# GpSimd's element-wise work moved to VectorE and ScalarE, which issue in the order of a trace-time clock

## The chip, the cores and the metric

The kernel runs on one core of a Trainium2 chip. Its time is the device time of one execution in microseconds (us); the lower the better. The engines are TensorE (PE, with its weight loads shown as PEld), VectorE (DVE), ScalarE (ACT), GpSimd (POOL) and SyncE (SP, which here issues most of the DMAs). In the instruction names `pb`, `pm` and `pt` are PSUM tiles, `s` is any of 69 SBUF slots of 128 x 512 float32, and `wst`, `whi`, `wlo` are a weight tile as loaded and its high and low halves.

## The reference

A decoder trunk of two layers on 512 tokens of width 1024. Each layer adds to the residual `h`, in this order, each after an RMS norm:

1. half a SwiGLU feed-forward of width 2816 (FFN1),
2. a mixer: one projection to 29 blocks of 128 columns, divided among a short gated convolution, HGRN2 (a gated linear recurrence, 6 heads of 64, in chunks of 64 tokens) and RWKV-7 (6 heads of 64), then an output projection,
3. cross-attention (4 heads) to 256 memory tokens,
4. a second half feed-forward (FFN2).

The parts of the mixer that the change touches:

```python
# RWKV-7: token shift, key, its normalisation, output
pf = pf + (p_prev - pf) * mu
kk = k * k_k
kk = kk / maximum(sqrt(sum(kk * kk)), 1e-12)
k  = k * (1 + (a - 1) * k_a)
state = state * w + (state @ -kk) outer (kk * a) + v outer k     # one token after the other
y = ((y - mean) * rsqrt(var + eps)) * ln_w + ln_b ; out = (y + bonus) * g
# HGRN2: gates
log_f = log_sigmoid(f) + log1p(lb * exp(min(-f, 80))) ; k = (1 - lb) * sigmoid(-f)
```

A final RMS norm ends the trunk. All is float32.

## The kernel before, in words

Activations lie with their features on the partitions, so a tile is 128 features of all 512 tokens. A product with a weight matrix is done in blocks of 128 output columns ("a weight product"). `load_w` (L413) loads a weight block by SP into `wst`; ACT copies it, rounded, into `whi`, and DVE forms the rest, `wlo`. For each of up to eight blocks of 128 inputs, three matmuls then run (high by high, high by low, low by high), so a product of 1024 inputs is 24 matmuls of 512 columns. `split` (L535) does the same to an activation: ACT makes the high part, DVE the low one.

The FFNs are a plain loop over such products (`ffn`, L640). `Norm.chunk` (L578) squares each finished block of `h` on ACT, adds it to a sum (on POOL, except in the first and the last norm) and splits the block for the next stage.

The mixer (`mix`, L1246) is a set of Python generators that are run side by side while the kernel is traced:

- `rw_inputs` (L767), one for each of three pairs of RWKV heads, makes decays, normalised keys and the products between tokens of a chunk. It ends with four DMAs of triangular blocks to DRAM (`Ad`) and marks its pair as done (`in0` to `in2`). `turned` (L726) transposes a tile in PE and copies it out of PSUM, here into `UV`.
- `rw_solve` (L906) loads all the blocks back (`G<-Ad`), inverts them on DVE by 60 small steps, stores the result (`Td<-G`), loads it back in 12 pieces (`s<-Td`) and completes it with matmuls; `rw_chain` then goes through the eight chunks one after the other with a state `S`, and `rw_post` normalises the result. These three run in sequence.
- `hgrn` does the three pairs of HGRN heads: `hg_gates` makes the decays, `hg_pair` the scores on six levels of a chunk (`scaled`, `scores`, `merge`). At its end it brings the parked `h` back from DRAM (`s<-hd`) and adds eight output products to the fill.
- `mem_normed` normalises the memory for cross-attention.
- The fill (`Fill`, L440) is a queue of weight products that need nothing of the generators: the 29 projections of the mixer, then keys and values of cross-attention.

`Fill.run` (L501) decides which of them issues next. A trace-time clock (`Clock`, L113) keeps, for each engine, the stretches in which it is taken to be busy, and for each buffer the time at which it is written and read, from a linear cost per operation; `Clock.pe` is PE's time. A generator yields a `Need`: tiles, keys of finished products, free slots (`room`) and free PSUM banks. One whose needs are met by the clock goes on; otherwise the fill does its next step of three matmuls. Those in the list `calm` (HGRN and the memory) are passed over while the clock sees more than 5 us of work on DVE beyond PE's time, and ask for three slots more.

PE's instructions are kept in the order in which they were traced (`tc.keep_in_program_order`). The order of the other engines, and of SP's queue, is chosen afterwards by the framework's own scheduler. Every engine then runs its instructions strictly in that fixed order on the chip. In the profile, all operations that go through the clock's wrapper have its line: L253 for DVE, ACT, POOL and DMAs, L302 for matmuls, L306 for transposes.

Of the kernel before, what the change touches and what calls it, by code (L numbers as in the profile page):

```python
# [17 lines left out]
SPACES = (bass.MemoryType.SB, bass.MemoryType.PSUM)  # L18

P = 128  # L20
# [59 lines left out]
class Slots:  # L80


    def __init__(self, pool, n):
        self.pool = pool
        self.free = deque(range(n))
        self.held = {}
        self.n = 0
        self.low = n

    def get(self, dt=F32):  # L90
        i = self.free.popleft()
        self.low = min(self.low, len(self.free))
        self.n += 1
        t = self.pool.tile([P, T], dt, name=f"s{i}_{self.n}", tag=f"s{i}", bufs=1)
        self.held[id(t)] = (i, t)
        return t
# [16 lines left out]
class Clock:  # L113
# [6 lines left out]
    def __init__(self):  # L120
        self.pe = 0.0
        self.mode = None
        self.func = None
        self.dma = 0.0
        self.busy = {e: [] for e in ("DVE", "ACT", "POOL")}
        self.buf = {}

# [5 lines left out]
    @staticmethod  # L133
    def box(x):
        if x.space not in SPACES:
# [14 lines left out]
    def last(self, name):  # L150
        return max((max(r[4], r[5]) for r in self.buf.get(name, ())), default=0.0)

# [34 lines left out]
    def note(self, engine, op, args, kw):  # L187
        aps = [x for x in args if type(x).__name__ == "AP"]
        outs = aps[:1] + [kw[k] for k in ("accum_out",) if k in kw]
        ins = aps[1:] + [v for k, v in kw.items() if k != "accum_out" and type(v).__name__ == "AP"]  # L190
        if op == "copy_predicated":
            ins.append(aps[0])
        t = max([self.when(x) for x in ins] + [self.when(x, True, engine == "PE") for x in outs]) + 0.06
        n = max(x.free_size() for x in (outs + ins)[:2])
        if engine == "PE":
            t = self.pe = max(self.pe, t - 0.06) + self.matmul(op, ins, kw)
            t += 0.2
        elif op == "dma_start":
            size = aps[0].size() * 4
            t = self.dma = max(t + 2.0, self.dma) + size / 300e3  # L200
        else:
            t = self.fit(engine, max(t, self.pe - 5), self.cost(engine, op, args, n, ins))
        for x in ins:
            self.use(x, t, False)
# [20 lines left out]
    def cost(self, engine, op, args, n, ins):  # L225
# [9 lines left out]
        if op == "tensor_tensor_scan":  # L235
            return 0.2 + 2.6e-3 * n
        if op == "copy_predicated":
            return 0.2 + 1.3e-3 * n
        return 0.17 + (1.5e-3 if op == "scalar_tensor_tensor" else 1.1e-3) * n


class Timed:
# [5 lines left out]
    def __getattr__(self, op):  # L248
# [3 lines left out]
        def call(*args, **kw):  # L252
            ins = fn(*args, **kw)  # L253
            clock.note(name, op, args, kw)
# [4 lines left out]
class Banks:  # L259
# [11 lines left out]
    def get(self, dt=F32):  # L271
        t = self.pool.tile(self.shape, dt, name=self.name, tag=self.name, bufs=self.n)
        i = len(self.names) - self.n
        if i >= 0:
            self.clock.use(t, self.clock.last(self.names[i]), False)
            self.clock.buf.pop(self.names[i], None)
# [6 lines left out]

class Need:


    def __init__(self, *aps, keys=(), room=0, banks=(), ahead=0.0):
        self.aps, self.keys, self.room, self.banks, self.ahead = aps, keys, room, banks, ahead


@with_exitstack
def trunk(ctx: ExitStack, tc: tile.TileContext, a, out, parts=("ffn1", "mix", "xa", "ffn2"), dbg=None):
# [30 lines left out]
    sl = Slots(spool, NSLOT)  # L323
# [25 lines left out]
    def send(key, t):  # L349

        away[key] = dram.tile([P, T], F32, name=key, tag=key)
# [58 lines left out]
    ve.tensor_scalar(oml, lbt, -1.0, 1.0, ALU.mult, ALU.add)  # L410

# [28 lines left out]
    class Fill:  # L440
# [60 lines left out]
        def run(self, *gens, calm=()):  # L501
# [9 lines left out]
            while todo:  # L511
                at = [ready(n, SPARE * c) for _, n, c in todo]
# [33 lines left out]
    def rms_sums(acc, n):  # L546
# [5 lines left out]
        r = tiny.tile([P, 4], F32, name="rms", tag="rms")  # L552
        ve.tensor_scalar(r[:, :k], ps[:, :k], 1.0 / D, EPS, ALU.mult, ALU.add)
        gp.tensor_tensor(r[:, :k], r[:, :k], mhalf.to_broadcast([P, k]), op=ALU.pow)
        rh = tiny.tile([P, 4], F32R, name="rmsh", tag="rmsh")
        rl = tiny.tile([P, 4], F32R, name="rmsl", tag="rmsl")
# [14 lines left out]
    class Norm:  # L571
# [6 lines left out]
        def chunk(self, d, adder=gp):  # L578
# [3 lines left out]
            else:  # L582
                sq = sl.get()
                se.activation(sq, h[d], AF.Square)
                adder.tensor_tensor(self.acc, self.acc, sq, op=ALU.add)
# [38 lines left out]
    def start(name, src):  # L624
# [10 lines left out]
        for d in range(ND):  # L635
            n.chunk(d, ve)
# [3 lines left out]
    def ffn(l, which, n, nxt, between=None):  # L640
# [13 lines left out]
        for f0, f1 in SLABS:  # L654
# [22 lines left out]
            for d in range(ND):  # L677
# [4 lines left out]
                if last:  # L682
                    nxt.chunk(d, ve if nxt.l is None else gp)
# [42 lines left out]
    def turned(x, low, dst):  # L726
# [4 lines left out]
        for hf in range(2):  # L731
# [12 lines left out]
            ve.tensor_copy(dst(high, 4 * hf + 1, 4 * hf + 1 + nw), pv[C:P, 0:nw, high, :])  # L744
            if hf:
                ve.tensor_copy(dst(high, 0, 1), pv[C:P, 3:4, high, :])
# [11 lines left out]
    def rw_shift(l, n, i, ps):  # L758
        t = evac(n, ps)
        dd = sl.get()  # L760
        gp.tensor_tensor(dd[:, 1:], t[:, :T - 1], t[:, 1:], op=ALU.subtract)
        gp.tensor_scalar(dd[:, 0:1], t[:, 0:1], -1.0, None, ALU.mult)
        ve.scalar_tensor_tensor(t, dd, col(l, "rwkv_mu", i), t, op0=ALU.mult, op1=ALU.add)
        sl.put(dd)
        return t

    def rw_inputs(l, n, st, p):  # L767
        UV, Z, lr, X = st["UV"], st["Z"], st["lr"], st["X"]
        cs = slice(p * P, (p + 1) * P)
        yield Need(keys=[(l, f"k{p}"), (l, "wa")], room=ROOMS[p])  # L770
# [15 lines left out]
        el = gp if p else ve  # L786
        el.tensor_tensor(lw, G, lw, op=ALU.subtract)

        kk = sl.get()
        ve.tensor_scalar(kk, k, col(l, "rwkv_k_k", p), None, ALU.mult)  # L790
# [14 lines left out]
        ve.tensor_scalar(t0, ag, 1.0, col(l, "rwkv_k_a", p), ALU.subtract, ALU.mult)  # L805
        ve.scalar_tensor_tensor(k, t0, 1.0, k, op0=ALU.add, op1=ALU.mult)
        el.tensor_tensor(ag, kk, ag, op=ALU.mult)
        pc = tiny.tile([P, NC_], F32, name="pc", tag=f"pc{p}", bufs=1)
        ve.tensor_copy(pc, c8(ep)[:, :, C - 1])
        st["pc"].append(pc)  # L810
        yield Need(keys=[(l, f"r{p}")], room=4)
        r = X[f"r{p}"]
        AR, BK, BKH, BKT = [], [], [], []
        for hf in range(2):
# [4 lines left out]
            gp.tensor_tensor(arv[:, :, 1, :], c8(r[:, tt]), c8(ep[:, tt]), op=ALU.mult)  # L819
# [3 lines left out]
            for j in range(2):  # L823
                js = half(j)
                ve.tensor_tensor(bkv[js, :, j, :], c8(ag[:, tt])[js], e[js], op=ALU.mult)
                gp.tensor_tensor(bkv[js, :, 1 - j, :], c8(k[:, tt])[js], e[js], op=ALU.mult)
            AR.append(ar)
            BK.append(bk)
        sl.put(lw, ag, kk, G)
# [5 lines left out]
        yield Need(room=5)  # L835
# [70 lines left out]
    def rw_solve(l, st):  # L906
# [6 lines left out]
        G = cpool.tile([P, H * H], F32, name="G", tag="G")  # L913
# [16 lines left out]
        sp.dma_start(Td, G[0:n, :])  # L930
        yield Need(room=6)
# [50 lines left out]
    def rw_chain(l, st):  # L982
# [13 lines left out]
        for c in range(NC_):  # L996
# [24 lines left out]
            if c < NC_ - 1:  # L1021
# [3 lines left out]
                S2 = tiny.tile([P, 3, C], F32, name="rwS", tag="rwS", bufs=3)  # L1025
# [17 lines left out]
    def rw_post(l, st, ys):  # L1043
# [17 lines left out]
        for p in range(3):  # L1061
# [3 lines left out]
            ve.tensor_scalar(y, y, col(l, "rwkv_ln_w", p), col(l, "rwkv_ln_b", p), ALU.mult, ALU.add)  # L1065
            gp.tensor_tensor(y, y, bon[p], op=ALU.add)
# [10 lines left out]
    def hg_gates(l, st, p):  # L1077
# [3 lines left out]
        x, m, e1, e2 = sl.get(), sl.get(), sl.get(), sl.get()  # L1081
        ve.tensor_scalar(x, f, -1.0, 80.0, ALU.mult, ALU.min)
# [3 lines left out]
        se.activation(e1, m, AF.Exp, scale=-1.0)  # L1086
        ve.tensor_tensor(x, x, m, op=ALU.subtract)
# [3 lines left out]
        se.activation(x, x, AF.Ln)  # L1091
        ve.scalar_tensor_tensor(e1, f, 0.0, e2, op0=ALU.min, op1=ALU.subtract)
        gp.tensor_tensor(m, m, x, op=ALU.add)
        gp.tensor_tensor(m, m, e1, op=ALU.add)

        k = sl.get()
        gp.tensor_tensor(k, e1, f, op=ALU.subtract)
        se.activation(k, k, AF.Exp)
        ve.tensor_scalar(k, k, oml[:, l, p:p + 1], None, ALU.mult)
# [503 lines left out]
```

## Time and profile before

| | |
|---|---|
| median of 3 runs | 2540.8 us (2539.44 to 2542.9) |
| the profiled execution | 2538.74 us, span 2536.9 us |
| granted TensorE clock, mean | 0.975 |
| busy: PE, DVE, ACT, POOL | 2436.8, 1405.4, 973.2, 271.1 us |
| HBM read and written | 228.39 MB and 12.06 MB |

The span runs from the first to the last instruction of the profiled execution. Stages by the span's time in us: FFN1 of layer 0 to about 383, its mixer to about 797, cross-attention to about 911, FFN2 and the FFN1 of layer 1 to about 1634, mixer to about 2046, cross-attention to about 2161, FFN2 and the last norm to the end.

An instruction's row gives line, engine, operation, output<-inputs, shape, count, busy time, mean ns of one, and the engine's idle time just before, with what ended it. A row of waits gives the waiting engine and tile, what released it, us in total, times, and the longest. A row of stretches gives start and end, length, for each engine its busy us and its instructions, then the granted clock as a share, the DMA engines' share and GB/s.

### The profile page before, as it was taken

To read this page: it belongs to the slowest core of one execution; us is meant where nothing else is said; L and a number is where in the kernel's file an instruction comes from. 1 tells how busy PE (TensorE), PEld (TensorE's weight loads), DVE (VectorE), ACT (ScalarE), POOL (GpSimd) and SP (SyncE) were. 2 spreads that over 40 slices of the span, in tenths; PEclk is the share of its full clock that TensorE was granted. 3 is DMA by queue.
4 is the path that set the end of the run, shared out by engine and by line. 5 is a ranking of instruction groups with operands and counts; after the bars stand their busy time and mean duration, and the time that the engine had idled before them with its cause. 6 is when DMAs were issued, how large, how long until landed. Compare 5 with 4: busy or idle time off the path is not lost.

```text
span 2536.9 us, 34159 instructions
## 1 busy us (share of the span) xinstructions
PE 2436.8 (96%) x13812; PEld 1993.4 (79%) x13812; DVE 1405.4 (55%) x2068; ACT 973.2 (38%) x1338; POOL 271.1 (11%) x250
## 2 busy tenths in 40 slices
PE   8999999799989999999999999988999899999997
PEld 6888887577868878888888888866877688788886
DVE  5444456777756554344554444576876566444444
ACT  4222235554554342222332222355454544322232
POOL 0000013411201010000100000243221111000000
PEclk9999999899999999999999999999999999999998
DMA  4333332134323133333323333412334222333322
GB/s 144 100 109 99 100 121 81 57 91 125 122 67 106 50 104 93 99 91 100 100 92 100 100 92 98 128 59 72 110 107 129 65 78 78 100 94 99 100 91 76
DMA packets 92012, 242.65 MB, mean 96 GB/s; under 512 B 21840, under 2 KB 24528, under 8 KB 91856
## 3 DMA queue, kind: packets, MB, share of 16 engines
q1 hardware_dynamic: 88544, 234.36, 29.9%
q10 hardware_dynamic: 3312, 6.12, 0.6%
q8 instruction: 109, 1.79, 0.3%
q14 instruction: 47, 0.39, 0.1%
HBM read 228.39 MB, written 12.06 MB: 95 GB/s over the span
## 4 chain that ended last, share of the span: by engine, by line
PE 82%; DVE 8%; ACT 4%; issue 3%; POOL 2%; DMA 1%; SPq 0%; DVEq 0%; ACTq 0%; POOLq 0%
PE pb L302 75%; DVE s L253 6%; PE pm L302 5%; ACT s L253 2%; POOL s L253 2%; PE pt L302 1%; ACT L253 1%; DVE wlo L253 1%; DVE G L253 1%; PE pm L306 1%; SPq L253 0%; DMA wst<-w_mix_in 0%; DMA hgate<-s 0%; ACT whi L253 0%; PE pt L306 0%
## 5 line engine op out<-in xcount | busy, mean ns | idle before, releaser
L302 PE MATMUL pb<-s,whi 128*128 128x512 f32 (+1 forms) x6160 | 1912.0, 392 | 22.3 <-DVE s L253 12.0
L302 PEld LDWEIGHTS pb<-s,whi 128*128 128x128 f32 x6160 | 1156.7, 191 | 276.1 <-issue 17.2
L302 PE MATMUL pb<-s,wlo 128*128 128x512 f32 (+1 forms) x3080 | 1196.8, 389 | 1.4 <-DVE wlo L253 1.4
L253 ACT ACTIVATE whi<-wst 128x1024 fp32r<-128x1024 f32 (+5 forms) x445 | 433.8, 976 | 1090.5 <-PE pb L302 735.9
L302 PEld LDWEIGHTS pb<-s,wlo 128*128 128x128 f32 x3080 | 586.6, 190 | 120.8 <-DVE wlo L253 3.4
L253 DVE TENSOR_TENSOR wlo<-wst,whi 128x1024 fp32r<-128x1024 f32 (+5 forms) x445 | 501.1, 1126 | 109.8 <-ACT whi L253 102.3
L253 DVE TENSOR_TENSOR s<-pb,s 128x512 f32<-128x512 f32 (+1 forms) x345 | 236.7, 689 | 524.5 <-PE pb L302 497.3
L253 ACT ACTIVATE s<-s 128x512 f32<-128x512 f32 (+2 forms) x458 | 284.4, 627 | 289.0 <-DVE s L253 229.0
L253 POOL TENSOR_TENSOR s<-s,s 128x512 f32<-128x512 f32 (+2 forms) x142 | 180.2, 1275 | 1591.1 <-ACT s L253 1348.8
L253 DVE TENSOR_TENSOR s<-s,s 128x512 f32<-128x512 f32 (+3 forms) x378 | 244.2, 655 | 77.0 <-ACT s L253 68.0
L253 DVE SCALAR_TENSOR_TENSOR s<-pb,s 128x512 f32<-128x512 f32 x96 | 66.4, 692 | 226.0 <-PE pb L302 226.0
L253 DVE SCALAR_TENSOR_TENSOR s<-s,vec,s 128x512 fp32r<-128x512 f32 (+2 forms) x100 | 115.9, 1161 | 36.9 <-POOL s L253 19.1
L253 ACT ACT_TABLE_LOAD x96 | 123.2, 1283 | 22.0 <-DVE s L253 17.3
L253 POOL TENSOR_TENSOR s<-s 128x256 f32<-128x256 f32 (+2 forms) x64 | 68.8, 1086 | 156.8 <-DVE s L253 98.3
L302 PEld LDWEIGHTS pm<-s,s 64*64 64x64 f32 (+2 forms) x1104 | 61.3, 156 | 18.4 <-issue 10.7
L302 PE MATMUL pm<-s,s 64*64 64x64 f32 (+2 forms) x1104 | 67.3, 246 | 8.4 <-ACT Z L253 3.4
L253 POOL TENSOR_TENSOR rms<-rms,mhalf 128x4 f32<-128x4 f32 (+1 forms) x10 | 10.4, 1040 | 449.6 <-DVE rms L253 449.6
L253 ACT ACTIVATE s<-s,vec 128x512 fp32r<-128x512 f32 (+1 forms) x72 | 50.9, 709 | 2.0 <-DMA s<-xT 2.0
L302 PE MATMUL pb<-whi,s 128*128 128x512 f32 x128 | 51.1, 441 | 0.0
L302 PEld LDWEIGHTS pm<-s 64*64 64x64 f32 (+1 forms) x1152 | 37.1, 140 | 8.6 <-issue 6.9
L302 PE MATMUL pm<-s 64*64 64x32 f32 (+1 forms) x1152 | 40.7, 224 | 0.0
L306 PE MATMUL pm<-cst,s 128*128 128x128 f32 x192 | 29.1, 294 | 6.7 <-ACT s L253 5.5
(105 smaller groups left out, 827.3 us busy)
## 6 DMA issues: line engine op xcount, KB each, us to landing
wst<-ffn_w_in SPq DMA_DIRECT2D x175, 512.0 KB, 3.5
wst<-w_mix_in SPq DMA_DIRECT2D x58, 512.0 KB, 3.5
wst<-ffn_w_out SPq DMA_DIRECT2D x64, 448.0 KB, 3.3
wst<-ffn_w_out SPq DMA_DIRECT2D x32, 512.0 KB, 3.5
wst<-xattn_wk SPq DMA_DIRECT2D x16, 512.0 KB, 3.5
wst<-xattn_wv SPq DMA_DIRECT2D x16, 512.0 KB, 3.7
wst<-xattn_wq SPq DMA_DIRECT2D x16, 512.0 KB, 3.4
wst<-xattn_wo SPq DMA_DIRECT2D x32, 256.0 KB, 2.6
```

Source lines behind the costliest of these rows:

```text
L253: ins = fn(*args, **kw)
L302: self.pin(nc.tensor.matmul(*args, **kw))
L306: self.pin(nc.tensor.transpose(*args, **kw))
```

## The change

1. *GpSimd's element-wise work.* All additions, subtractions and products of whole tiles go from POOL to DVE. POOL keeps the power of -0.5 of the norms' sums and the memsets.
2. *Fewer and other steps.* The token shift `t + (prev - t) * mu` is done as `t * (1 - mu)` on ACT and one multiply-add on DVE (`omu` is made once), without the two POOL steps. The key's norm is `exp(-0.5 * ln(max(sum, 1e-24)))` in place of square root, maximum, logarithm and exponential. `1 + (a - 1) * k_a` is one ACT step (`omka` is made once).
3. *DVE's work to ACT.* Scalings by a column (`k_k`, `1 - lb`, `hgrn_norm`), the affine step with `ln_w` and `ln_b`, and all PSUM copies of `turned` are done by ACT.
4. *The order.* The clock notes for each DVE and ACT instruction (ACT's DMA issues too) when it takes it to start; at the end `issue_in_order` sorts each engine's instructions by that time and chains them by manual dependencies. The clock is refined: new costs for DVE, reuse of buffers (`renew`), readers of one PSUM bank one after the other, DMAs fitted into gaps. The memory's loads are no longer kept in program order.
5. *Who waits.* `rw_inputs` joins the `calm` list, ahead of `hgrn`; `mem_normed` leaves it and asks for more slots. `hgrn`'s gates wait for `in2`, that is for all RWKV inputs, and yield in several places.

```diff
+def issue_in_order(tc, clock):
+    dep = mybir.DependencyInfo(mybir.DependencyClass.NoSync, mybir.DependencyReason.DATA)
+    for q in clock.queue.values():
+        q = [x[2].ins for x in sorted(q, key=lambda x: x[:2])]
+        for a, b in zip(q, q[1:]):
+            tc.add_manual_dep(b, a.name, dep, reason="issue_in_order")
...
         else:
-            t = self.fit(engine, max(t, self.pe - 5), self.cost(engine, op, args, n, ins))
+            cost = self.cost(engine, op, args, n, reads)
+            t = self.fit(engine, max(t, self.pe - 5), cost)
+            first = t - cost
+            t += 0.08
+            if engine in self.queue:
+                self.queue[engine].append((first, len(self.queue[engine]), ins))
...
-        return 0.17 + (1.5e-3 if op == "scalar_tensor_tensor" else 1.1e-3) * n
+        return 0.08 + (1.15e-3 if op == "scalar_tensor_tensor" else 1.05e-3) * n
...
     def rw_shift(l, n, i, ps):
         t = evac(n, ps)
-        dd = sl.get()
-        gp.tensor_tensor(dd[:, 1:], t[:, :T - 1], t[:, 1:], op=ALU.subtract)
-        gp.tensor_scalar(dd[:, 0:1], t[:, 0:1], -1.0, None, ALU.mult)
-        ve.scalar_tensor_tensor(t, dd, col(l, "rwkv_mu", i), t, op0=ALU.mult, op1=ALU.add)
-        sl.put(dd)
-        return t
+        x = sl.get()
+        se.activation(x, t, AF.Copy, scale=omu[:, l * 11 + i:l * 11 + i + 1])
+        ve.scalar_tensor_tensor(x[:, 1:], t[:, :T - 1], col(l, "rwkv_mu", i), x[:, 1:], op0=ALU.mult, op1=ALU.add)
+        sl.put(t)
+        return x
...
             se.copy(dst(low, 4 * hf, 4 * hf + 4), pv[0:C, :, low, :])
             nw = 3 + (hf == 0)
-            ve.tensor_copy(dst(high, 4 * hf + 1, 4 * hf + 1 + nw), pv[C:P, 0:nw, high, :])
+            se.copy(dst(high, 4 * hf + 1, 4 * hf + 1 + nw), pv[C:P, 0:nw, high, :])
...
         ps = head_sum(t0)
-        se.activation(t0, ps, AF.Sqrt)
-        ve.tensor_scalar(t0, t0, 1e-12, None, ALU.max)
+        ve.tensor_scalar(t0, ps, 1e-24, None, ALU.max)
         se.activation(t0, t0, AF.Ln)
-        se.activation(t0, t0, AF.Exp, scale=-1.0)
-        el.tensor_tensor(kk, kk, t0, op=ALU.mult)
+        se.activation(t0, t0, AF.Exp, scale=-0.5)
+        ve.tensor_tensor(kk, kk, t0, op=ALU.mult)
...
-            yield Need(keys=[(l, f"hg{p}")], room=11 if p == 2 else 7)
-            gates.append(hg_gates(l, st, p))
+            yield Need(keys=[(l, f"hg{p}"), (l, "in2")], room=11 if p == 2 else 7)
+            gates.append((yield from hg_gates(l, st, p)))
...
-            gp.tensor_tensor(wb[:, :, 1, :], bb[:, :, 1, :], ref, op=ALU.subtract)
+            ve.tensor_tensor(wb[:, :, 1, :], bb[:, :, 1, :], ref, op=ALU.subtract)
...
-        F.run(*[rw_inputs(l, n, st, p) for p in range(3)],
-              seq(rw_solve(l, st), rw_chain(l, st), rw_post(l, st, ya)), calm=(hgrn(), mem_normed()))
+        F.run(seq(rw_solve(l, st), rw_chain(l, st), rw_post(l, st, ya)), mem_normed(),
+              calm=[rw_inputs(l, n, st, p) for p in range(3)] + [hgrn()])
...
-        (gp if d % 3 == 2 else ve).tensor_tensor(n.scaled[d], n.scaled[d], n.rstd, op=ALU.mult)
+        ve.tensor_tensor(n.scaled[d], n.scaled[d], n.rstd, op=ALU.mult)
         (sp if d % 2 else se).dma_start(out[:, d, :], n.scaled[d])
+    issue_in_order(tc, clock)
```

More of the change, by code (lines that the diff above doesn't have):

```diff
@@ L80, with __init__ @@
 class Slots:
-    def __init__(self, pool, n):
+    def __init__(self, pool, n, clock):
         self.pool = pool
+        self.clock = clock
         self.free = deque(range(n))
@@ L94, in get @@
         t = self.pool.tile([P, T], dt, name=f"s{i}_{self.n}", tag=f"s{i}", bufs=1)
+        self.clock.renew(t, f"s{i}")
         self.held[id(t)] = (i, t)
@@ L123, in __init__ @@
         self.func = None
-        self.dma = 0.0
-        self.busy = {e: [] for e in ("DVE", "ACT", "POOL")}
+        self.busy = {e: [] for e in ("DVE", "ACT", "POOL", "DMA")}
         self.buf = {}
+        self.names = {}
+        self.fresh = set()
+        self.queue = {e: [] for e in ("DVE", "ACT")}
     @staticmethod
@@ L134, in box @@
     def box(x):
-        if x.space not in SPACES:
+        if x.space != bass.MemoryType.SB:
             return 0, INF, 0, INF
@@ L151, in last, with renew, tile @@
         return max((max(r[4], r[5]) for r in self.buf.get(name, ())), default=0.0)
+    def renew(self, x, old):
+        t = self.last(old)
+        self.buf.pop(old, None)
+        self.buf[self.key(x)] = [(0, INF, 0, INF, t, t)]
+        self.fresh.add(self.key(x))
+    def tile(self, pool, shape, dt, name, bufs):
+        t = pool.tile(shape, dt, name=name, tag=name, bufs=bufs)
+        names = self.names.setdefault(name, [])
+        names.append(t.name)
+        if len(names) > bufs:
+            self.renew(t, names[-1 - bufs])
+        return t
     def use(self, x, t, write):
@@ L253, in call @@
             ins = fn(*args, **kw)
-            clock.note(name, op, args, kw)
+            clock.note(name, op, args, kw, ins)
             return ins
@@ L271, in get @@
     def get(self, dt=F32):
[L272 to L276, printed above, removed]
+        t = self.clock.tile(self.pool, self.shape, dt, self.name, self.n)
         self.names.append(t.name)
@@ L349, in send @@
     def send(key, t):
-        away[key] = dram.tile([P, T], F32, name=key, tag=key)
+        away[key] = clock.tile(dram, [P, T], F32, key, 1)
         sp.dma_start(away[key], t)
@@ L410, in trunk @@
     ve.tensor_scalar(oml, lbt, -1.0, 1.0, ALU.mult, ALU.add)
+    omu = cpool.tile([P, 2 * 11], F32, name="omu", tag="omu")
+    for l in range(L):
+        o = l * VL + VOFF["rwkv_mu"]
+        ve.tensor_scalar(omu[:, l * 11:l * 11 + 11], vec[:, o:o + 11], -1.0, 1.0, ALU.mult, ALU.add)
+    omka = cpool.tile([P, 2 * 3], F32, name="omka", tag="omka")
+    for l in range(L):
+        o = l * VL + VOFF["rwkv_k_a"]
+        ve.tensor_scalar(omka[:, l * 3:l * 3 + 3], vec[:, o:o + 3], -1.0, 1.0, ALU.mult, ALU.add)
     def load_w(src, cols, piece=1024, between=None):
@@ L511, in run @@
             while todo:
-                at = [ready(n, SPARE * c) for _, n, c in todo]
+                at = [ready(n, SPARE * (c and n.spare)) for _, n, c in todo]
                 busy = clock.backlog("DVE") > CALM
@@ L930, in rw_solve @@
         sp.dma_start(Td, G[0:n, :])
+        F.done.add((l, "solved"))
         yield Need(room=6)
```

132 lines of the change are left out of this document (73 added, 59 removed).

## The prediction

> **What bounds the kernel now.** I read the page's head and its chain of work first, then the busy times by stage, the waits of TensorE (PE), and the timeline where its longest wait stands. The stages below are FFN, mix, cross-attention, two FFNs, mix, attention, FFN.
>
> ```profile
> span 2536.9 us, 34159 instructions
> PE 2436.8 (96%) x13812; PEld 1993.4 (79%) x13812; DVE 1405.4 (55%) x2068; ACT 973.2 (38%) x1338; POOL 271.1 (11%) x250
> ...
> PE 82%; DVE 8%; ACT 4%; issue 3%; POOL 2%; DMA 1%; SPq 0%; DVEq 0%; ACTq 0%; POOLq 0%
> ```
>
> ```profile
> 403.00:757.00 354.00, 319.60 (x2875) 251.87 (x2872) 250.15 (x460) 189.51 (x263) 85.69 (x86) 0.93 0.29 88
> 924.00:1654.00 730.00, 730.00 (x3237) 604.23 (x3236) 341.46 (x390) 216.46 (x265) 29.12 (x22) 1.00 0.32 99
> 1654.00:2006.00 352.00, 317.28 (x2873) 250.41 (x2871) 249.23 (x458) 189.11 (x263) 85.57 (x86) 0.93 0.29 89
> ```
>
> The columns after the stretch and its length are PE, weight loads, VectorE (DVE), ScalarE (ACT), GpSimd (POOL), then the granted clock. In the FFNs PE is busy 730.00 of 730.00 us at clock 1.00: nothing done on the other engines can shorten them. Only the two mixes are open: PE idles 354.00 - 319.60 = 34.4 us in the first and 34.7 us in the second, and the clock loses up to 0.07 x 354 = 25 us in each, some 10 of it inside the idle time itself (estimate: a little under a third of the idle at half clock). So 2 x (34.5 + 15) = 99 us is all that a perfect order could bring. Attention has only single waits of 1 us at its edges.
>
> Who ends PE's waits in the first mix (us in total, times, longest), in three windows, 403 to 500, 500 to 600, 600 to 757:
>
> ```profile
> PE pm L302 <- DVE UV L253: 10.1, 2, 8.6
> PE pm L306 <- ACT s L253: 2.8, 1, 2.8
> ...
> PE pm L302 <- ACT s L253: 4.6, 2, 4.1
> PE pm L302 <- ACT Z L253: 1.7, 1, 1.7
> ...
> PE pt L302 <- DVE s L253: 7.9, 2, 5.3
> PE pt L302 <- issue: 2.1, 1, 2.1
> ```
>
> (The 4.1 within the 4.6 straddles two windows and ends near 600; one more of 3.75 is shown below.) These are a few long waits, not many short ones. The longest, in the timeline:
>
> ```profile
> 444.13 2.12 DVE L253 SCALAR_TENSOR_TENSOR s<-s,s 128x256 f32<-128x256 f32 x2
> 446.33 3.43 POOL L253 TENSOR_TENSOR s<-s,s 64x256 f32<-64x256 f32 x4 [0.63 <-DVE s L253]
> 454.79 0.43 DVE L253 COPY UV<-pm 64x256 f32<-64x256 f32 x1
> 455.27 3.37 PE L302 MATMUL pm<-s,lr 64*128 64x512 f32 x4 [8.63 <-DVE UV L253]
> 456.00:463.00 7.00, 7.00 (x21) 3.80 (x21) 4.83 (x7) 5.58 (x7) 2.60 (x3) 0.56 0.14 32
> ```
>
> PE is pinned to the order of the trace-time clock. Its next matmul needs a PSUM bank that a 0.43 us copy on DVE frees, and that copy stands at 454.79, behind some 10 us of RWKV products that DVE shares with POOL. The order that DVE runs is not the order that PE's order was made for. Afterwards PE runs at 0.56 for 7 us, so the wait costs 8.6 + 3.1 us.
>
> **The change part by part.** The durations that price it (mean ns of one is the number after the busy time):
>
> ```profile
> L253 POOL TENSOR_TENSOR s<-s,s 128x512 f32<-128x512 f32 x106 | 151.0, 1428 | 1561.9 <-ACT s L253 1342.2 <-DVE s L253 219.2
> L253 POOL TENSOR_TENSOR s<-s 128x256 f32<-128x256 f32 x36 | 31.1, 876 | 100.6 <-PE pm L302 51.3 <-DVE s L253 42.0 <-PE pt L302 7.2
> L253 POOL TENSOR_TENSOR s<-s 128x511 f32<-128x511 f32 x22 | 29.2, 1328 | 43.7 <-DVE s L253 43.7
> L253 POOL TENSOR_TENSOR s<-s,s 64x256 f32<-64x256 f32 x24 | 19.8, 824 | 20.6 <-DVE s L253 19.2
> L253 DVE TENSOR_TENSOR s<-s,s 128x512 f32<-128x512 f32 x154 | 109.2, 712 | 54.1 <-ACT s L253 46.3
> L253 DVE TENSOR_TENSOR s<-s,s 128x256 f32<-128x256 f32 x72 | 29.3, 438 | 5.9 <-ACT s L253 5.9
> L253 DVE TENSOR_TENSOR s<-s,s 64x256 f32<-64x256 f32 x24 | 18.4, 767 | 0.2
> L253 DVE SCALAR_TENSOR_TENSOR s<-s,vec,s 128x512 fp32r<-128x512 f32 x64 | 86.5, 1354 | 17.1 <-ACT s L253 15.5
> L253 DVE TENSOR_SCALAR s<-s,vec 128x512 f32<-128x512 f32 x28 | 14.1, 505 | 12.0 <-POOL s L253 11.6
> L253 ACT ACTIVATE s<-s,vec 128x512 f32<-128x512 f32 x8 | 5.7, 710 | 0.0
> L253 ACT COPY s<-pm 64x256 f32<-64x256 f32 x24 | 8.2, 360 | 18.7 <-PE pm L306 16.1 <-PE pm L302 2.7
> L253 ACT ACT_TABLE_LOAD x96 | 123.2, 1283 | 22.0 <-DVE s L253 17.3
> ```
>
> *POOL to DVE.* 106 full-width and some 6 more of its products at 0.71 us make 80 us, and about 72 of 256 columns at 0.44 us make 32: DVE gets 112 us. *DVE to ACT.* 54 PSUM copies of the transposes (about 18 us in all at 0.22 to 0.43 each), 24 of the 28 scalings at 0.505 (12 us) and 6 more scalings go over: DVE loses some 35. *Contention.* Half-width products that take 438 ns at 256 columns take 767 while POOL runs its own 824; the 64 split steps, mostly beside POOL's sum of squares, take 1354 where a full-width product takes 712. With POOL silent that gives back 64 x 0.64 = 41, 24 x 0.33 = 8, and from the like forms about 20 more: some 70 us. So 112 - 35 - 70 leaves DVE at about 1412 us, as now; without any relief it would be 1405 + 77 = 1482, and with the mean of the undisturbed steps being lower still (the 712 and 438 hold some disturbed ones), some 1390. I take 1410.
>
> [...]
>
> *ACT.* 22 token shifts become one ACT scaling each (0.71) instead of 1.33 and a one-column step on POOL: 15.6 us; 18 scalings at 0.71 make 13; 12 affine steps, not in this trace, lie between 0.63 (a full-width step without operands, estimate from this 0.71) and 0.9, say 9; the copies, at 0.36 for the largest of three sizes, 16. Six Sqrt steps go, some 4 us, with between none and two table loads each, up to 12 x 1.28 = 15 us. ACT ends between 1008 and 1023, 40%: it does not bind, its latencies stand beside PE's fill work (each weight product is 24 matmuls, some 5.4 us).
>
> *The order.* DVE and ACT are chained in the order of the clock that also orders PE. It costs no instruction. What it can close is the wait between the two orders. Per mix: the UV wait (its copy is on ACT now) 8.6, of which I take 6, since DVE still has the same products to do, and its slow clock 3; the ACT and Z waits (2.8 + 1.7 and small ones, 6 in all) half, 3; the DVE waits of the state chain, where
>
> ```profile
> 654.15 2.65 DVE L253 TENSOR_TENSOR s<-s 128x256 f32<-128x256 f32 x3
> 658.46 0.34 DVE L253 TENSOR_TENSOR s<-Z,pt 128x192 f32<-128x192 f32 x1
> 653.00:667.00 14.00, 8.71 (x90) 7.79 (x88) 11.01 (x22) 5.49 (x9) 4.93 (x6) 0.63 0.33 111
> ```
>
> three HGRN subtractions at 0.88 beside POOL stand ahead of the 0.34 us addition that the chain needs, 5.3 + 2.1, half, 3.5, and 2.5 of 5 for the clock at 0.63. The wait of 4.1 stays, because its cause is elsewhere:
>
> ```profile
> 587.42 5.75 SPq L253 DMA_DIRECT2D s<-Td  x12
> 598.09 1.06 ACT L253 ACTIVATE whi<-wst 128x1024 fp32r<-128x1024 f32 x1 [2.51 <-DMA wst<-w_mix_in]
> ```
>
> Twelve small loads of the solved blocks hold SP's queue 5.75 us, the weight load waits behind them, ACT behind that load, and the clock does not know the queue. The last wait, 3.75 for the RWKV post-processing, and 2.6 of the 7.9 come where weight products run out; with PE quicker they can grow: -2. Shorter GpSimd steps on the RWKV path (1.43 to 0.71, some ten per head pair) keep that path up with PE: +1. Sum per mix 6 + 3 + 3 + 3.5 + 2.5 - 2 + 1 = 17, both 34.
>
> *Elsewhere.* The splits ahead of attention and FFN2 (1354 to 712) save about 1 us twice. At the end
>
> ```profile
> 2526.63 5.83 DVE L253 TENSOR_TENSOR s<-s,s 128x512 f32<-128x512 f32 x6 [2.54 <-ACT s L253]
> ```
>
> six scalings beside POOL's two take 0.97 each; eight at 0.71 take 5.7: nothing to 1 us. Two small tables (omu, omka) are 4 short operations under the first weight loads: nothing. Total 34 + 2 + 1 = 37.
>
> *Held back.* RWKV inputs now wait while DVE has over 5 us of work, and HGRN waits for all RWKV inputs. Behind the first stand solve, state chain and post-processing; in exchange HGRN no longer takes DVE from them. While DVE is full PE takes weight products, 29 of which, 157 us, are there for the inputs' 120. So I cost it at nothing; without that cover PE idles for each us of the delay (rival 3). A DVE step that waits for a late DMA, such as the solve's, holds every weight split behind it; DVE runs in one fixed order before too, so the price is the 4.1 above, and I leave it. No DMA changes queue. Memory loads are no longer pinned on SP, and ACT's own issues (parking, half of the outputs) take their place in its chain: between -1 and +1 us, nothing taken, since they run under weight products.
>
> [...] The rows (0.56 over 7 us) give 3.1, and by them I go.
>
> The profiled execution took 2538.7 us (span 2536.9 and 1.8 around it), 2 under the median of 2540.8. 2538.7 - 37 gives 2502; I say 2501, the calibrated costs of the clock being one small help more.
>
> **The rivals.**
> 1. *The waits nearly all close.* With the true order known PE finds weight products for every wait. Of 99 us some 75 to 90 would go: about 2456. For it: waits are few and long, and DVE and ACT have room (250 and 190 of 354 us). Against: 4.1 + 3.75 + 2.6 of 34 are not of that kind.
> 2. *New waits take the place.* DVE's 250 us stay, PE pays the same waits one product later: 2540, no change. Against it, the bank that PE waited for is freed by ACT, which idled there.
> 3. *Slower: HGRN comes too late.*
>
> ```profile
> 471.57 0.43 DVE L253 TENSOR_SCALAR s<-s 128x512 f32<-128x512 f32 x1 [1.16 <-ACT s L253]
> 752.23 1.09 PE L302 MATMUL pb<-s,whi 128*128 128x512 f32 x2 [3.75 <-DVE s L253]
> L253 SPq DMA_DIRECT2D Ad<-s x12: 326/444/1224, 440.1 to 521.0; - x12
> L253 SPq DMA_DIRECT2D s<-hd x8: 320/402/613, 679.7 to 690.3; - x8
> L253 ACT ACTIVATE dec<-s x3: 202/214/216, 499.7 to 650.7; 128x8 f32<-128x8 f32 x3
> ```
>
> The rows are the first step of HGRN's first gates, the first matmul of the mix's last products, the stores of the RWKV inputs' blocks, the loads that follow HGRN's last block, and the last step of each gate. The first gates take 471.6 to 499.7, 28 us, some 22 without POOL; from there to the last block, at 679.7, are 180 us. RWKV inputs end some 15 us after 521.0. If the gates start only then, 536 + 22 + 180 + 16 for HGRN's eight output products (9 matmuls of 0.23 each) is 754, where the mix's last products begin at 752 now: there is no slack at all. Each us beyond, by longer HGRN or later inputs, is paid twice, once a layer. Held back by 15 us more: 2538.7 + 2 x 15 = 2569. It decides once the inputs end later than now with HGRN as long as now. Against: HGRN loses some ten POOL steps per head pair at 0.5 to 0.7 us each, 15 to 20 us in all, and its rivals on DVE, and the inputs are forecast to end sooner.
>
> **How the numbers follow.** Two executions differ by 0.1%, so 0.2% (5 us) is about what can be told from no change. Forecast (2475 to 2530) 0.55; only a few us won (2530 to 2535) 0.06; rival 1 0.13; rival 2 0.08; rival 3 0.18. Faster 0.74, same 0.08, slower 0.18. The low end, 2458, reaches rival 1; the high end, 2556, takes in no change and half of rival 3, which is also about what DVE without relief would cost if a quarter of its 77 us fell on PE's path (2538.7 + 19). The likeliest case alone is 2475 to 2530.
>
> **What would show it.** POOL near 15 us busy; DVE within 30 of 1405; ACT between 1000 and 1025; split steps at 0.75. FFN stretches unchanged. Mix idle near 20 each, no wait on a UV copy, the wait after the Td loads still there. Wrong if HGRN's unparking ends past 735, or if PE waits for DVE in the first 100 us of a mix more than now.

## The result, and the profile after

The changed kernel takes 2483.6 us (median, 2480.3 to 2484.7) against 2540.8 before: a ratio of 0.977, 95% interval 0.976 to 0.979, or 57 us less. The profiled execution of it took 2484.7 us, span 2482.9.

The page of the changed kernel, its head and its chain of work by engine:

```profile
span 2482.9 us, 33542 instructions
PE 2410.2 (97%) x13812; PEld 1977.9 (80%) x13812; DVE 1383.0 (56%) x2172; ACT 997.0 (40%) x1426; POOL 15.7 (1%) x22
...
PE 89%; DVE 5%; ACT 4%; issue 1%; DMA 0%; SPq 0%; POOLq 0%; DVEq 0%; ACTq 0%
```

GpSimd has 15.7 us of work left, and DVE is 22 us shorter although it took the rest. PE does the same 13812 matmuls in 27 us less busy time: that is the clock, granted at 0.985 in place of 0.975. The whole first mix, from the first matmuls of its stage to the first of the next, before and then after (columns as in the prediction: length, PE, weight loads, DVE, ACT, POOL, granted clock):

```profile
382.00:790.00 408.00, 373.60 (x3119) 296.28 (x3118) 288.30 (x506) 214.87 (x299) 100.69 (x99) 0.94 0.30 93
```

```profile
388.00:757.00 369.00, 354.87 (x3119) 284.20 (x3118) 278.72 (x535) 232.16 (x344) 3.67 (x5) 0.99 0.33 104
```

Of the 39 us that this mix lost, 20.3 are PE's idle time (34.4 to 14.1) and 18.7 are PE's busy time for the same 3119 matmuls (clock 0.94 to 0.99). In the second mix the idle time fell by 20.6 us and the busy time by 14.1. Stage by stage, from the first matmuls of one stage to those of the next, in us (the first column is only a part of its stage, between two of its matmuls; the last ends some 12 us before PE's last matmul):

| | FFN1, layer 0, first part | mix 0 | attention 0 | FFN2, layer 0 | FFN1, layer 1 | mix 1 | attention 1 | FFN2, layer 1 |
|---|---|---|---|---|---|---|---|---|
| before | 152.5 | 408.2 | 115.4 | 366.4 | 360.9 | 406.8 | 115.4 | 358.4 |
| after | 157.5 | 369.1 | 121.4 | 366.9 | 360.9 | 372.0 | 120.1 | 362.6 |

So the mixes won 74 us and the other stages lost 20. What they lost to is in PE's waits for a weight's low half, in the whole kernel before and then after, and in the timeline of the changed kernel at the step from mix to attention:

```profile
PE pb L302 <- DVE wlo L253: 1.4, 2, 1.2
```

```profile
L341 PE MATMUL pb<-s,wlo 128*128 128x512 f32 (+1 forms) x3080 | 1196.1, 388 | 30.0 <-DVE wlo L286 30.0
```

```profile
755.94 1.04 ACT L286 ACTIVATE whi<-wst 128x1024 fp32r<-128x1024 f32 x1
758.85 0.69 DVE L286 TENSOR_TENSOR s<-s,s 128x512 f32<-128x512 f32 x1 [0.69 <-ACT s L286]
759.46 0.75 DVE L286 SCALAR_TENSOR_TENSOR s<-s,vec,s 128x512 fp32r<-128x512 f32 x1
760.13 2.35 DVE L286 TENSOR_TENSOR wlo<-wst,whi 128x1024 fp32r<-128x1024 f32 x2
761.40 0.80 PE L341 MATMUL pb<-s,wlo 128*128 128x512 f32 x1 [3.53 <-DVE wlo L286]
```

PE waited 1.4 us in the whole kernel before for a weight's low half; now it waits 30.0. High halves are there by 757, but the low half that PE needs stands on DVE behind the last stage's work: the sum of squares (758.85) and the split of the last block of `h` (759.46), the first of which waited 0.69 us for ACT. PE, which has everything else, stops for 3.53 us. This happens at both edges of each attention, and once (3.58) in FFN1 of layer 0. These five make 17.7 of the 30.0 us; 9.9 more are four waits for a low half inside the mixes (2.86 and 2.1 in each).

The durations that the prediction used, and PE's longest waits from 440 to 740 in the first mix (us in total, times, longest):

```profile
L286 DVE TENSOR_TENSOR s<-s,s 128x512 f32<-128x512 f32 x266 | 181.8, 690 | 70.1 <-ACT s L286 64.1
L286 DVE SCALAR_TENSOR_TENSOR s<-s,vec,s 128x512 fp32r<-128x512 f32 x64 | 47.9, 751 | 4.5 <-ACT s L286 4.5
L286 DVE TENSOR_TENSOR s<-s,s 64x256 f32<-64x256 f32 x48 | 18.1, 415 | 0.2
L286 ACT ACT_TABLE_LOAD x84 | 107.8, 1283 | 3.1 <-PEq L1647 1.7
```

```profile
PE pm L341 <- DVE s L286: 5.3, 1, 5.3
PE pb L341 <- DVE wlo L286: 2.1, 1, 2.1
PE pt L341 <- DVE rwS L286: 1.1, 2, 0.6
```

The 8.6 us on a `UV` copy are gone, and so are the state chain's 5.3 and 2.1. One wait of 5.3 is left, from 592 to 597.

### The profile page after: what moved, and what is told of

Its sections match the earlier page's. It is cut to its first block, busy times and chain, and to the rows that moved or that the text cites. A ratio compares the mean times of both kernels' runs of the same rounds, so it can differ in the third digit from the quotient of the medians.

```text
span 2482.9 us, 33542 instructions
## 1 busy us (share of the span) xinstructions
PE 2410.2 (97%) x13812; PEld 1977.9 (80%) x13812; DVE 1383.0 (56%) x2172; ACT 997.0 (40%) x1426; POOL 15.7 (1%) x22
## 4 chain that ended last, share of the span: by engine, by line
PE 89%; DVE 5%; ACT 4%; issue 1%; DMA 0%; SPq 0%; POOLq 0%; DVEq 0%; ACTq 0%
PE pb L341 80%; PE pm L341 6%; DVE s L286 4%; ACT s L286 3%; PE pt L341 1%; ACT L286 1%; PE pm L345 1%; DVE wlo L286 1%; ACT whi L286 0%; PE pt L345 0%; DMA s<-xT 0%; DVE G L286 0%; SPq L286 0%; ACT UV L286 0%; POOLq L1654 0%
## 5 line engine op out<-in xcount | busy, mean ns | idle before, releaser
L286 ACT ACTIVATE whi<-wst 128x1024 fp32r<-128x1024 f32 (+5 forms) x445 | 424.2, 969 | 394.7 <-PE pb L341 135.2
L286 DVE TENSOR_TENSOR wlo<-wst,whi 128x1024 fp32r<-128x1024 f32 (+5 forms) x445 | 495.9, 1116 | 153.2 <-ACT whi L286 152.4
L286 DVE TENSOR_TENSOR s<-s,s 128x512 f32<-128x512 f32 (+3 forms) x526 | 318.0, 622 | 144.2 <-ACT s L286 136.0
L286 DVE SCALAR_TENSOR_TENSOR s<-s,vec,s 128x512 fp32r<-128x512 f32 (+2 forms) x100 | 74.6, 750 | 9.4 <-ACT s L286 9.0
L286 ACT ACTIVATE s<-s,vec 128x512 fp32r<-128x512 f32 (+1 forms) x90 | 64.4, 719 | 3.3 <-DMA s<-xT 1.7
L286 ACT COPY s<-pm 64x256 f32<-64x256 f32 (+3 forms) x69 | 23.3, 358 | 76.9 <-PE pm L341 66.0
L286 ACT ACTIVATE s<-pb 128x512 fp32r<-128x512 f32 x32 | 18.8, 596 | 37.0 <-PE pb L341 36.8
L286 DVE TENSOR_TENSOR s<-s 128x256 f32<-128x256 f32 (+1 forms) x79 | 31.4, 436 | 0.1
L341 PEld LDWEIGHTS pb<-whi,s 128*128 128x128 f32 x128 | 24.0, 188 | 6.0
```

The costliest lines, as they stand in the source:

```text
L341: self.pin(nc.tensor.matmul(*args, **kw))
```

## The experiments

Two theories stood against each other at first. By the *order theory*, the prediction's, the gain comes from chaining DVE and ACT to the clock that also orders PE. By the *GpSimd theory* it comes from the moved operations: with GpSimd silent DVE's steps are shorter (the 64 split steps took 1354 ns before and 751 after). Each ratio is against runs of the kernel before on the same chip, next to it in time.

**Each half alone.** `e1_moves_only` is the kernel before with parts 1 to 3 of the change (the operations) and without 4 and 5; `e2_order_only` is the changed kernel with the operations as before.

```diff
# e1, on the kernel before
-        def chunk(self, d, adder=gp):
+        def chunk(self, d):
-        (gp if d % 3 == 2 else ve).tensor_tensor(n.scaled[d], ...)
+        ve.tensor_tensor(n.scaled[d], ...)
...
# e2, on the changed kernel: the same lines the other way round
```

> Before with the operations moved and rewritten (GpSimd's work on VectorE, scalings and copies on ScalarE), but with its clock, its order by the framework's scheduler and its list of calm generators. If the order is what won the 57 us: 2520 to 2542, the long waits still there at other places. [...] Both theories have VectorE busy near 1385 us and the split steps at 0.75 us.

> After with all the operations put back where they were before (GpSimd, VectorE), but with the new clock, the chained order of VectorE and ScalarE, and the new lists of who is held back. Order theory: 2490 to 2510, the waits of 8.6 and 5.3 us gone. GpSimd theory: 2525 to 2545, since chained VectorE waits for GpSimd's slow steps as before.

Measured: e1 2467.9 us (ratio 0.972, 0.970 to 0.974), e2 2483.4 (0.978, 0.977 to 0.979). Either half alone brings about as much as both, or more, so neither theory is whole, and something in the full change costs. The longest waits of the first mix in e1, then in e2:

```profile
PE pm L302 <- ACT UV L253: 4.7, 1, 4.7
PE pt L302 <- ACT UV L253: 3.5, 1, 3.5
```

```profile
PE pb L341 <- DVE wlo L286: 7.6, 4, 3.9
PE pm L341 <- DVE s L286: 2.7, 4, 1.0
```

With the moves alone `UV` copies are still waited for, now on ACT, in smaller pieces. With the order alone (parts 4 and 5) they aren't waited for at all, though they stand on DVE as before. The moves alone also shorten FFN2 of layer 0 from 366.4 to 360.9 us and mixes to 378.0 each; the order alone shortens mixes to 375.6 and 378.7, leaves FFN2 at 366.7 and has attention at 114.9 in both layers.

**Without the chain, without the holding back, without both.**

```diff
# e3: the changed kernel without the chains
-    issue_in_order(tc, clock)
# e4: without the holding back
-            yield Need(keys=[(l, f"hg{p}"), (l, "in2")], room=11 if p == 2 else 7)
+            yield Need(keys=[(l, f"hg{p}")], room=11 if p == 2 else 7)
-        F.run(seq(rw_solve(l, st), rw_chain(l, st), rw_post(l, st, ya)), mem_normed(),
-              calm=[rw_inputs(l, n, st, p) for p in range(3)] + [hgrn()])
+        F.run(*[rw_inputs(l, n, st, p) for p in range(3)],
+              seq(rw_solve(l, st), rw_chain(l, st), rw_post(l, st, ya)), calm=(hgrn(), mem_normed()))
# e5: both edits
```

> After without the chaining of VectorE and ScalarE alone: clock, moved operations and held-back generators stay; PE's order is unchanged from after. Order theory: 2515 to 2545, and long waits on VectorE return. GpSimd theory: 2480 to 2495. In both the five waits of 2 to 3.6 us on the low half of a weight tile, which stand in after and not in before, go, if they come from the chaining.

> After with the generators run as before: RWKV inputs not held back and first in the list, HGRN not waiting for them, memory among the calm ones. If holding back is needed: 2505 to 2530, with VectorE's queue in the first 100 us of a mix longer than PE can cover. If the order alone carries it: 2480 to 2495.

> After without the chaining and without holding back: the moved operations and the new clock remain, the generators run as before. If the 37 us that the chaining costs and the 33 that the holding costs are separate: 2405 to 2425, with mixes near 352 us and attention at 115. If the short mixes (354 us) of the run without holding need the chained order: mixes of 365 to 378, 2440 to 2470.

Measured: e3 2446.3 us (0.963, 0.962 to 0.965), e4 2450.3 (0.965, 0.963 to 0.966), e5 2461.8 (0.970, 0.969 to 0.972). Taking out either is worth 33 to 37 us, more than either theory allowed, but taking out both does not bring the sum: the two get in each other's way. Their stages, in us:

| | mix 0 | mix 1 | attention 0 | FFN2, layer 0 | FFN2, layer 1 |
|---|---|---|---|---|---|
| after (chain and hold) | 369.1 | 372.0 | 121.4 | 366.9 | 362.6 |
| e3 (hold, no chain) | 366.0 | 367.5 | 115.2 | 361.2 | 356.4 |
| e4 (chain, no hold) | 354.5 | 354.0 | 120.1 | 367.9 | 361.5 |
| e5 (neither) | 374.4 | 373.7 | 115.2 | 360.9 | 355.5 |

The chain has two effects with opposite signs. Outside the mixes it costs 28 us (e4 against e5) and 32 us (after against e3) in the profiled executions. Inside the mixes it gains 20 us each without the holding back (374 to 354) and loses 3 to 5 each with it. Holding back helps an unchained mix by 6 to 8 us and harms a chained one by 15 to 18.

**The edges.** The clock places a DVE step at most 5 us ahead of PE. `e6_ahead_10` makes that 10, in the changed kernel, and e7 the same without the holding back.

```diff
-            t = self.fit(engine, max(t, self.pe - 5), cost)
+            t = self.fit(engine, max(t, self.pe - 10), cost)
```

> After with one number changed: the clock may place work of VectorE and ScalarE up to 10 us before PE's time instead of 5, and so chain the weight splits earlier. If the chaining costs 30 us because the splits of weights at a stage's edge stand behind that stage's last steps, placed at most 5 us ahead: 2448 to 2460, attention back from 121 to 115 us and the waits of 2 to 3.6 us on the low half gone. If any fixed order costs this: 2478 to 2488.

> After with both: chained, 10 us ahead, and no holding back. If both costs are as told and separate: 2412 to 2426. If the larger distance spoils the order inside the mixes: 2430 to 2455, with mixes over 358 us.

Measured: e6 2476.1 us (0.976, 0.974 to 0.978), e7 2448.2 (0.965, 0.963 to 0.966). The edge in FFN1 of layer 0 goes (157.5 to 150.4 us), those around attention stay (120.4 both in e6). e7 is no faster than e4, and neither of its cases holds: the mixes stay at 356 us, and the edges don't go. The bound explains the one, not the others: `fit` places a step only in time that the steps traced earlier have left free, and the next stage's first splits are traced after the last stage's work. Two kernels without the holding back go at that in different ways. `e9_no_hold_loose` leaves all weight splits out of the chains; `e10_edges`, on e7, keeps them chained and traces the next stage's first weights earlier.

```diff
# e9, on e4
-            if engine in self.queue:
+            if engine in self.queue and not self.loose:      # loose: set while load_w splits
# e10, on e7
+        ask = queue_q(l, nxt)                # attention's weight products join the fill ...
+        F.until((l, f"o0{ND - 1}"))          # ... before the mixer's last products have run
-        F.finish()
...
+        F.until((l, f"xo1{ND - 3}"))
+        F.load(AHEAD)
+        w = load_w(a["ffn2_w_in"][l, 0], 1024)   # FFN2's first weight, two products early
```

> The changed kernel without the holding back, and with the weight splits (the copy to whi and the subtraction to wlo) left out of the chains, so that the scheduler may put them ahead of work that the clock noted earlier; all other DVE and ACT work stays chained. Chained splits theory (the 3.5 us waits for a low half where stages meet come from weight splits chained behind the last stage's work): attention back from 120 to 115 us, FFN2 from 368 and 361.5 to 361 and 355.5, FFN1 of layer 0 from 157 to 151, mixes still 354: 2450 - 28 = about 2420 us. Rival (the mixes' gain lives on the chained splits, since PE's fill work needs a weight at the time the clock says): the edges go, but the mixes rise above 358 us each, 2430 to 2455.

> The changed kernel without the holding back, everything chained, the clock's bound at 10 us ahead of PE, and the next stage's first weights loaded and split in the trace before the last two products of the mixer's and of the attention's output. If the waits for a low half where stages meet come from the order in which these splits are traced: attention 115 to 116 us, FFN2 361 and 356, mixes 354 to 356, about 2425 us. If they come from the scheduler or from the loads themselves, nothing changes against the same kernel without this step: 2448 us.

Measured: e9 2436.6 us (0.959, 0.958 to 0.961), e10 2426.1 (0.955, 0.954 to 0.956). Both clear the edges: attention is 114.9 us in both, FFN2 360.9 in layer 0 of both, 356.2 and 355.5 in layer 1. But e9 pays for it in the mixes, 364.3 and 360.7 where e10 has 356.5 and 356.1, and e4 354.5 and 354.0. That a mix needs its weights split at the time that PE's order counts on fits this. So the edges go when the next stage's first weights and products are traced earlier, and the splits can stay chained. The group for a low half, the whole first mix, and PE's longest waits from 383 to 860, in e10:

```profile
L341 PE MATMUL pb<-s,wlo 128*128 128x512 f32 (+1 forms) x3080 | 1189.6, 386 | 6.9 <-DVE wlo L286 6.6
```

```profile
383.00:739.00 356.00, 350.34 (x3117) 279.54 (x3116) 277.24 (x535) 231.37 (x344) 2.74 (x5) 1.00 0.33 107
```

```profile
PE pb L341 <- DVE wlo L286: 2.5, 2, 2.1
PE pm L341 <- DVE s L286: 1.4, 1, 1.4
PE pm L345 <- DVE s L286: 1.0, 1, 1.0
```

The mix is at clock 1.00 with 5.7 us of idle time, and this kernel, 114 us under the one before, is the fastest measured.

The chain alone doesn't make the edges around attention, though. e2 is chained too, and its attention takes 114.9 us. The same edge there:

```profile
759.05 1.21 DVE L286 TENSOR_TENSOR wlo<-wst,whi 128x1024 fp32r<-128x1024 f32 x1
759.93 1.48 POOL L286 TENSOR_TENSOR s<-s,s 128x512 f32<-128x512 f32 x1 [1.96 <-ACT s L286]
760.43 1.52 DVE L286 SCALAR_TENSOR_TENSOR s<-s,vec,s 128x512 fp32r<-128x512 f32 x1 [0.18 <-ACT s L286]
760.94 0.61 PE L341 MATMUL pb<-s,whi 128*128 128x512 f32 x2
```

With the operations of before, GpSimd adds the squares (759.93). The first low half for attention is made at 759.05, ahead of the split of the last block of `h`, and PE comes to attention at 760.94 without a wait. In the changed kernel DVE's gaps between the last stage's steps are 0.64 to 0.70 us long from 752 to 759, and a low half takes 1.2. So this wait comes of the chain and the moved operations together. That `fit` found no gap long enough is the likely reason and wasn't tried by itself. The wait in FFN1 of layer 0 is there in e2 as well (3.65 us).

**What holding back costs.** `e8_hgrn_free` drops HGRN's wait for `in2` alone; `e12_inputs_free` keeps that wait and takes the RWKV inputs out of the `calm` list, first in the order as before.

```diff
# e12
-        F.run(seq(rw_solve(l, st), rw_chain(l, st), rw_post(l, st, ya)), mem_normed(),
-              calm=[rw_inputs(l, n, st, p) for p in range(3)] + [hgrn()])
+        F.run(*[rw_inputs(l, n, st, p) for p in range(3)],
+              seq(rw_solve(l, st), rw_chain(l, st), rw_post(l, st, ya)), mem_normed(), calm=[hgrn()])
```

> After with HGRN's gates free to start before the RWKV inputs are done; the inputs stay in the calm list. If HGRN's late start is what the holding costs (rival 3 of the prediction, its slack used up): 2448 to 2460. If the inputs' being held back costs it: 2475 to 2490. If both share: 2460 to 2475.

> The changed kernel, chained, with HGRN's wait for all RWKV inputs kept, but the RWKV inputs no longer held back: they go first in the list as in the kernel before and are not in the calm list. If the holding back of the inputs makes up the 28 us that are left between the changed kernel and the one without any holding back (HGRN's wait was worth 5): mixes 356 to 358, 2453 to 2458 us. Rival: holding costs through HGRN as well, and only both together bring it back: mixes 363 to 370, 2468 to 2480 us.

Measured: e8 2478.2 us (0.977, 0.975 to 0.979), e12 2477.3 (0.975, 0.974 to 0.977): by their ratios 1 and 5 us of the 33, inside the intervals, with mixes of 368 to 369 in both. The rest comes only in e4, which drops both and also puts the memory back into the `calm` list, as neither of these does; that third difference wasn't tried by itself. The loads of `h` that follow HGRN's last block show where a single edit leaves HGRN; after, e8, e12, e4:

```profile
L286 SPq DMA_DIRECT2D s<-hd x8: 319/320/585, 664.6 to 683.5; - x8
```

```profile
L286 SPq DMA_DIRECT2D s<-hd x8: 319/339/1257, 667.9 to 683.9; - x8
```

```profile
L286 SPq DMA_DIRECT2D s<-hd x8: 320/323/424, 666.7 to 687.4; - x8
```

```profile
L286 SPq DMA_DIRECT2D s<-hd x8: 319/326/989, 641.8 to 655.1; - x8
```

With mixes that start within 2 us of each other (387 to 389), HGRN ends near 666 as long as either the inputs or HGRN is held, and at 642 when neither is. The first mix's end moves with it, from 757 to 741. That a late HGRN is what lengthens the mix fits these four but wasn't tried by itself, and it isn't all that counts: in e11, below, these loads start at 641.5 in a mix of 374 us.

**The last corner.** `e11_order_no_hold_ops_back` has the chain and the refined clock, no holding back, and the operations of before: e2 with e4's edit.

```diff
# on e2, the F.run list and HGRN's Need as in e4
```

> The changed kernel without the holding back and with the operations of before (GpSimd's adds and products, DVE's copies and scalings): the chains and the refined clock alone. If the chains carry the mixes' gain by themselves, as they did beside the holding back, where the moved operations were worth nothing: 2445 to 2455 us, mixes 354 to 358. If the moved operations are worth something once nothing is held back (they brought 73 us when done alone in the kernel before): 2470 to 2500 us, mixes 365 to 380.

Measured: 2472.0 us (0.973, 0.972 to 0.975), mixes 374.1 and 373.3. Beside this, e4 with the moves has 354. So the moves are worth 22 us once nothing is held back, and nothing (e2 against after) while it is. The stages show how this nothing comes about: against e2 the changed kernel's mixes are 6.5 and 6.7 us shorter and its attentions 6.5 and 5.2 longer. Alone, in the kernel before, the moves were worth 71. The order's share is as fluid: 68 alone, and 18 on top of the moves (e1 to e4), with the loss at the edges in it.

## Why the prediction was right, and where it wasn't

The direction, the likeliest side and the range held: 2483.6 lies in the likeliest case's own range, 17 us under the number. The sum of 37 is right to 20 us partly by luck, since the mixes won 74 where 34 was forecast, and the edges lost 20 where a gain of 2 was. In each mix the sum had 11.5 us for waits and 5.5 for the clock; the first mix won 20.3 and 18.7, the second 20.6 and 14.1. By its steps:

- *Operations.* POOL 15.7 us (15 forecast). DVE 1383, against 1410, below even the 1390 named as the low bound: the relief was larger, since DVE takes 690 ns for a full-width product where 712 was used, and 415 for the 64x256 products that had taken 767. ACT 997, just under 1000: 12 table loads fewer, the whole 15 us that stood there as "up to" (8 of them go with the order alone, in e2, which keeps the square roots, and 2 with the moves alone, in e1, so dropping the square roots is not what saved most of them). Split steps 751 ns, as forecast. The shorter steps go with the moved operations: in e1, with the moves alone, the 64x256 products take 417 ns and the split steps 748; in e2, where GpSimd works on, 695 and 1234. Why a DVE step takes longer while GpSimd works isn't shown by any run.
- *The `UV` wait.* 6 of 8.6 was taken; all of it went. e2, and e11 without the holding back, show that the chained order with the refined clock does this without the moves, and e1 that moving the copies to ACT alone only shortens it.
- *The clock term was mis-sized most.* 5.5 us per mix were given for it, and PE's busy time fell by 18.7 and 14.1. The bound of 15 per mix, and with it "99 us is all that a perfect order could bring", was too low as well. By the records 6.8 of the first mix's 34.4 us of idle time stood at half rate (a granted clock of 0.50), which loses half of them, so 3.4 us and not the estimated 10 come off the 25, and some 22 are left. In e10 PE's busy time fell by 23.3 in the first mix and by 19.9 in the second. The trace's records of the granted clock have 51 us at half rate in the first mix before and 10 after, in stretches of 3.4, 6.8 or 10.2 us; e10's first mix has a mean clock of 1.00. The wait of 8.6 us before, which ended at 455.27, had 10.2 us at half rate about its end:

```profile
452.00:462.20 10.20, 6.93 (x13) 3.81 (x13) 7.74 (x12) 6.35 (x9) 2.77 (x5) 0.50 0.20 56
```

In the changed kernel, matmuls that end a wait, each with the stretch behind it:

```profile
428.29 0.50 PE L341 MATMUL pb<-s,wlo 128*128 128x512 f32 x1 [2.86 <-DVE wlo L286]
429.13:432.54 3.41, 3.41 (x12) 2.52 (x11) 3.22 (x5) 2.79 (x6) 0.00 (x0) 0.50 0.48 154
...
730.40:734.00 3.60, 3.60 (x16) 2.98 (x17) 1.60 (x3) 0.71 (x1) 0.00 (x0) 1.00 0.59 181
...
1949.94 0.51 PE L341 MATMUL pb<-s,wlo 128*128 128x512 f32 x1 [2.10 <-DVE wlo L286]
1951.48:1954.89 3.41, 3.41 (x10) 2.65 (x9) 0.26 (x1) 0.74 (x1) 0.00 (x0) 0.50 0.47 175
```

  Behind the wait of 2.86 us, which ended at 428.29, came a stretch of 3.41 us at half rate. The wait of 2.1 at the end of the mix had none behind it in the first layer (730.40, at full rate), and one of 3.41 us in the second, beginning 1.5 us after the wait had ended. So in these two kernels the clock's loss came in whole stretches, and a shortened wait dropped one or more of them or none; the prediction gave 5.5 us for 12.5 closed us instead of this. What sets the start and the length of a stretch isn't shown.
- *The wait that "stays".* A wait of 5.27 us stood from 592 to 597 after, where one was to stay, but the reason given, SP's queue held by the twelve `s<-Td` loads, does not hold. The loads in e4 and PE's longest wait there from 440 to 740, then the loads in e12 and the wait that stands long after them:

```profile
L286 SPq DMA_DIRECT2D s<-Td x12: 337/449/451, 570.2 to 575.5; - x12
...
PE pb L341 <- ACT whi L286: 1.4, 1, 1.4
```

```profile
L286 SPq DMA_DIRECT2D s<-Td x12: 330/448/452, 566.2 to 571.5; - x12
...
594.11 1.31 PE L341 MATMUL pb<-s,whi 128*128 128x256 f32 x2 [4.92 <-ACT s L286]
```

  The loads hold the queue as long in e4, at no cost. Nor is it the wait of before: that one was for ACT, this one is for DVE:

```profile
590.88 1.12 PE L341 MATMUL pm<-s 64*64 64x32 f32 x32
...
595.71 0.88 DVE L286 SCALAR_TENSOR_TENSOR s<-s,vec,rmem 128x256 f32<-128x256 f32 x2
596.50 0.72 DVE L286 COPY_PREDICATED s<-cst,pm 128x256 f32<-128x256 int32 x1
597.27 2.03 PE L341 MATMUL pm<-s,s 64*64 64x64 f32 x32 [5.27 <-DVE s L286]
```

  PE had written `pm` by 592.0. The copy out of it stood on DVE behind steps of the memory's normalisation (`rmem`) and splits, and came without idle time of DVE before it; PE went on when it ended. Whether the copy could have gone earlier wasn't tried.
- *The step that failed* is in "Held back": "DVE runs in one fixed order before too, so the price is the 4.1 above". One fixed order is not like another: that of the framework's scheduler has no waits for `wlo` at the edges (before, e3, e5). In the order of the clock, with the moved operations on DVE, the weight splits of a new stage stand behind the old stage's last work, at 28 to 32 us (e4 against e5, after against e3). It is rival 2's mechanism, a new wait in the place of the old, but outside the mixes, where the prediction counted only small gains.
- *FFN stretches* without an edge are unchanged (360.9 both). The 1 us twice for splits ahead of attention and FFN2 was low: e1, without a chain, gains 5.5 and 2.9 at FFN2; in the changed kernel the edges take that back.
- *Rival 3.* The gates of HGRN were held back, to 522.6 for the last step of the first gates, against 499.7 before (of these 23 us 6 are the mix's later start); yet the unparking ended at 683.5, before the 690.3 of the kernel before and far from 735.

```profile
L286 ACT ACTIVATE dec<-s x3: 197/199/216, 522.6 to 646.7; 128x8 f32<-128x8 f32 x3
```

  From there to HGRN's end took 142 us (522.6 to 664.6) in place of 180, where 15 to 20 us of relief were counted. Holding back did have a price, 33 us against e4 over both mixes, but it was paid out of a larger gain and is seen only against a kernel that isn't held back. That it runs through HGRN, as the rival has it, isn't shown: freeing HGRN alone (e8) brings 1 us by the ratios.

## What to carry to other kernels

When one engine's order is made by a clock, chaining the other engines to the same clock can remove waits between two orders (here the 8.6 us on `UV`, in e2); but then work that is traced late can run late where the engine is full, as the weight splits did here once DVE had the sums as well. So the first loads and splits of the next stage should be traced ahead of the last stage's small work. Two changes that each help can cancel (holding back and chaining here; moving work and holding back): time the corners, not the sum. When waits of several us on TensorE are shortened, count the half-rate clock behind them as well: beside 20.3 us of idle time the first mix here won 18.7 of PE's busy time, and the second 14.1 beside 20.6.

## What the hardware showed that was not expected

- In the traces before and after, stretches at a granted clock of 0.50 came only in lengths of 3.4 us and its multiples (apart from the one at a kernel's end), up to 13.7 in the mixes before. In the changed kernel one began 1.5 us after the wait that it followed, and one, at 1910.5, had only waits of 0.53 and 0.51 us just before it.
- A full-width ACT step took 629 ns in the changed kernel without a column operand, 713 with `omu`, 0.08 us more, and 817 with two (`omka` and `vec`), another 0.10; the prediction had only bounds, 0.63 and 0.9, for a step with two:

```profile
L286 ACT ACTIVATE s<-s 128x512 f32<-128x512 f32 x328 | 202.6, 629 | 515.8 <-DVE s L286 514.3
L286 ACT ACTIVATE s<-s,omu 128x512 f32<-128x512 f32 x22 | 15.3, 713 | 16.3 <-DVE s L286 16.3
L286 ACT ACTIVATE s<-s,omka,vec 128x512 f32<-128x512 f32 x6 | 4.9, 817 | 1.5 <-DVE s L286 1.2
```
